# One layer of a hybrid sparse and dilated attention decoder: part of VectorE's work moved later in its queue, and the down projection's products regrouped by stationary operand

## The chip, the cores and the metric

The kernel runs on one core of a Trainium2 chip. The metric is the device time of one execution in microseconds (us), median over runs. The kernel before was run three times: 410.62 us median, 409.74 to 410.94. One further execution was profiled, and all rows below come from it.

## The reference, cut to what matters

```python
# x: (1, 256, 1024) float32; D_FF = 2816; 8 + 12 heads of 64 columns
h = rmsnorm(x, g_mix)
proj = h @ w_in                     # 5656 columns: q_a, kv_a, gate_a, qkv_b, merge_logits
kc = compress(kv_a[:, :, 0], pe_cmp_k, w_cmp_k1, w_cmp_k2)   # gelu(blocks @ w1) @ w2
vc = compress(kv_a[:, :, 1], pe_cmp_v, w_cmp_v1, w_cmp_v2)
gate_a = sigmoid(gate_a)
o_a = nsa_attention(q_a, kc, vc, ..., gate_a)                # compressed + selected + window
o_b = dilated_attention(qkv_b)
mixed = sigmoid(ga) * (o_a @ w_proj_nsa) + sigmoid(gb) * (o_b @ w_proj_dil)
x = x + mixed @ w_out
h = rmsnorm(x, g_ffn)
u, gate = split(h @ w_up)                                    # 2 x 2816 columns
x = x + (gelu(causal_conv3(u)) * gate) @ w_down
return rmsnorm(x, g_final)
```

## The kernel before, in words

**Three products for one.** Matmuls run in fp32r. Each operand is split into a high part (its fp32r copy, made by ScalarE) and a low part (the rest, a subtraction on VectorE), and a product is three matmuls: high by high, high by low, low by high. Names with h or hi (`whi`, `hTh`, `KH`, `ah`) are high parts, those with l or lo (`wlo`, `hTl`, `KL`, `al`) low parts.

**Units.** The weights are cut into 64 units, nearly all of 1 MB, in a list `units` that one loop (from L1084) goes through in order; i is the number of the unit. For unit i the loop starts the load of unit i+4 into one of three `raw` buffers, splits later units (`hi_of(i + 2)` on ScalarE, `lo_of(i + 1)` on VectorE, L128 and L132), issues the unit's matmuls (`u.mm`), and then its evacuation from PSUM (`u.evac`). Between these stand single steps under conditions on i. Nothing reorders afterwards: each engine carries its instructions out in the order in which the loop writes them, so a step that is written earlier delays all that is behind it on that engine. A `raw` buffer is loaded again when the low part of the unit in it is made.

**The units around the change.** Units 0 (the compression's keys and values) and 1 (the other keys of the first mixer), 2 (values and gates), 3 and 4 (`qa`, the queries of the first mixer), 5, 7 and 9 (`qb`, queries of the second), 6 and 8 (`w_cmp_k1` and `w_cmp_v1`, the compression's first layer, `mm_w1`, L421), 10 to 12 (`kb`). Steps among them:

- `ev_ka` (L384, unit 1's evacuation, called at i == 3): keys into `k`, four copies into `KH` (each group's keys in its own and in the other half of the partitions), two subtractions into `KL`.
- `xc_tile`, `split_cmp` (L325): high and low part of the compression's input, `XC`.
- `q_parts` (L436; L443 and L444): high and low part of the queries, `QS`, two heads of each group a call; `gates_of` (L429): the gates' sigmoid.
- `cmp_sum` (L721): adds the two halves of the compression's first layer (`ph`, in one of the two buffers of PSUM tag d) into `S2`; `cmp_fold` (L731) multiplies that on TensorE (L735).
- The first attention item, head 0, has its scores (`qk`, L840 and L842) behind unit 8, its softmax (`sm`, `sm2`, L854 to L873) on VectorE and ScalarE, and its transposes (`tr`, L882) behind unit 9.

PSUM tag d has two buffers. While `ph` holds one, units 5, 7 and 9 share the other, and each needs the evacuation (`ev_qb`, L450) of the one before.

**The feed-forward part.** From unit 31 on (`NFIRST`) the list is, for each j, two up units of 256 columns (weights stationary, `hTh` and `hTl` moving) and the down unit of j - 2 (activations `ah`, `al` stationary, weights moving). A down unit multiplies 256 rows of `w_down` into four PSUM banks (`ffn["y"]`: tiles `ps_s` and two `ps_t`), for two halves t of the sequence and two halves ch of the columns, in matmuls of 256 moving columns. `parts` (L160) writes the order: for each PSUM piece the products of `whi` with `ah` and `al` in turn (L177), and behind all pieces those of `wlo` (L182). `rt["kick"]` asks `parts` for one more matmul of 64 columns ahead of a unit (L172), whose result isn't used. The last two down units run piece by piece in `last` (L1180).

Of the kernel before, what the change touches and what calls it, by code (L numbers as in the profile page):

```python
# [14 lines left out]
AF = mybir.ActivationFunctionType  # L15
# [6 lines left out]
NF = DFF // 256  # L22
# [71 lines left out]
def build(ctx, tc, a, out):  # L94
# [67 lines left out]
    def parts(groups, w_stationary=True, start=True, stop=True):  # L162


        banks = set()
        kick = rt.pop("kick", None)
        if kick:

            (wh, _, xh, _), po = groups[0][2][0], groups[0][1]
            l, r = (wh, xh) if w_stationary else (xh, wh)  # L170
            po = pd([64], kick) if len(kick) == 1 else po[:, :64]
            T.matmul(po, l, r[:, :64], start=True, stop=True, skip_group_check=True)  # L172
        for (bank, po, ks) in groups:
            for (wh, wl, xh, xl) in ks:
                for x in (xh, xl):
                    l, r = (wh, x) if w_stationary else (x, wh)
                    T.matmul(po, l, r, start=start and bank not in banks, stop=False, skip_group_check=True)  # L177
                    banks.add(bank)
        for (bank, po, ks) in groups:
            for n, (wh, wl, xh, xl) in enumerate(ks):  # L180
                l, r = (wl, xh) if w_stationary else (xh, wl)
                T.matmul(po, l, r, start=False, stop=stop and n == len(ks) - 1, skip_group_check=True)  # L182

    def w3(u, k):
        n = u.n // k
        return (u.hi[:, u.o:u.o + u.n].rearrange("p (k c) -> p k c", k=k),
                u.lo[:, u.o:u.o + u.n].rearrange("p (k c) -> p k c", k=k))
# [40 lines left out]
    def bc(R, n):  # L228
        return R[:, None, :].to_broadcast([128, n, R.shape[-1]])
# [154 lines left out]
    def ev_ka(u):  # L384
        k = att.tile([128, 2, S], F32, name="E", tag="E", bufs=2)
        V.tensor_tensor(out=k, in0=u.p, in1=bc(rt["R"], 2), op=OP.mult)
        for g in range(2):
            h = slice(g * 64, g * 64 + 64)
            o = slice(64 - g * 64, 128 - g * 64)
            A.activation(KH[h, g], k[h], AF.Copy)  # L390
            V.tensor_sub(KL[h, g], k[h], KH.bitcast(F32)[h, g])
            A.activation(KH[o, g], k[h], AF.Copy)

    units.append(Unit(2048, lambda u: None, ev_ka))

# [40 lines left out]
    def q_parts(i):  # L436
        for g in range(2):
            h = slice(g * 64, g * 64 + 64)
            o = slice(64 - g * 64, 128 - g * 64)
            for j in (2 * i, 2 * i + 1):  # L440

                q, f = g * 4 + j, 1.0 / SLOPE_A[g * 4 + j]
                A.activation(M["QS"][h, q], qa[h, j], AF.Copy, scale=f)  # L443
                V.scalar_tensor_tensor(M["QS"][o, q], qa[h, j], f, M["QS"].bitcast(F32)[h, q],  # L444
                                       op0=OP.mult, op1=OP.subtract)
# [167 lines left out]
        return f  # L613

    def mm_down_part(u, j, tcs, c0=0, c1=512, own=None):
        wh, wl = w3(u, 2)
        h, l = ffn["a", j]
        parts([((t, ch), ffn["y"][t][ch][:, b:e] if own is None else own,
                [(wh[:, kt, ch * 512 + b:ch * 512 + e], wl[:, kt, ch * 512 + b:ch * 512 + e],
                  h[:, kt, t * 128:t * 128 + 128], l[:, kt, t * 128:t * 128 + 128]) for kt in range(2)])  # L620
               for (t, ch) in tcs for b, e in ([(0, 256), (256, 512)] if c1 - c0 == 512 else [(c0, c1)])],
              False, start=j == (0 if own is None else NF - 2), stop=j == NF - 1)

    def mm_down(j):
        def f(u):
            if j == 0:
                s2 = pd([2, 512], "s")
                ta = pd([512], "t")
                tb = pd([512], "t")
                ffn["y"] = [[s2[:, 0], s2[:, 1]], [ta, tb]]  # L630
            if j < NF - 2:
                rt["kick"] = "od"[j % 2]
                mm_down_part(u, j, [(t, ch) for t in range(2) for ch in range(2)])
        return f

# [368 lines left out]
    def load_to(n):  # L1004
        nonlocal loaded
        while loaded < min(n, len(units)):
            load_unit(units[loaded])
            loaded += 1
# [71 lines left out]
    def at(i):  # L1080
        return items.get(i, [])

    post = []
    for i, u in enumerate(units):  # L1084
        load_to(i + LA)
        for it in at(i - 3):
            it.fin()
        for it in at(i - 2):
# [18 lines left out]
        if i == 3:  # L1107
            hi_of(5)
            mixer_tiles()
            u1.evac(u1)  # L1110
            xc_tile()
            split_cmp(0)
            split_cmp(1)
        if i == 5:
            q_parts(0)
            gates_of()
        if i == 6:
            q_parts(1)
        if i == 9:
            cmp_sum()  # L1120
        if i == 11:
            cmp_kv_ev()
        if i == 14:
# [37 lines left out]
            u.pre(u)  # L1161
        if u.evac and i not in (0, 1, NFIRST):
            u.evac(u)
        if u.pre:
            post.append(post_g(len([q for q in units[:i] if q.pre])))
        for it in at(i - 2):
# [72 lines left out]
```

## Time and profile before

| | |
|---|---|
| median of 3 runs | 410.62 us |
| lowest, highest | 409.74, 410.94 us |
| profiled execution, its own time | 411.17 us |
| its span (first to last instruction) | 409.4 us |
| TensorE busy | 397.6 us, 97% |
| VectorE busy | 291.1 us, 71% |
| ScalarE busy | 212.2 us, 52% |
| mean granted TensorE clock | 0.991 of 2.4 GHz |

The difference of 1.77 us between the profiled execution's time and its span lies before its first and behind its last instruction. Matmuls are pipelined: one takes some 280 ns from start to end, and the next starts some 115 ns after it, so the distance from start to start is the cost, not the mean duration.

### The profile page before, as it was taken

The page shows a single profiled execution, that of the slowest core. Times are in us where ns is not written, and L with a number is a line of the kernel's source. Part 1 is how long each engine was busy: PE and PEld are TensorE (multiplying, and loading weights), DVE is VectorE, ACT ScalarE, POOL GpSimd, SP SyncE. Part 2 cuts the span into 40 slices and gives each one's busy share as a digit, 9 for nine tenths or more (in the row PEclk, how much of TensorE's full clock was granted, in tenths as well). Part 3 has the DMA queues.
Part 4 walks back from the last instruction along what each step waited for, and adds up shares of the span by engine and source line. Part 5 has one row for each costly group of instructions (what it writes and reads, how often), then busy time and mean ns, then how long its engine had stood idle before and what let it go on. Part 6 is the DMA issues. An engine that isn't in the chain of part 4 may idle for free.

```text
span 409.4 us, 8037 instructions
## 1 busy us (share of the span) xinstructions
PE 397.6 (97%) x3421; PEld 386.2 (94%) x3421; DVE 291.1 (71%) x486; ACT 212.2 (52%) x293; POOL 31.2 (8%) x58
## 2 busy tenths in 40 slices
PE   9999899999999999999999999999999999999993
PEld 6999898999998989999999999999999999999992
DVE  5878977887686756648889399685584764946853
ACT  6768552457654534681652766355255452653512
POOL 7100000000000000042143000000000000000012
PEclk9999899999999999999999999999999999999997
DMA  8963764324632343252555436753735727448002
GB/s 316 391 242 113 285 219 162 148 103 170 243 105 102 118 161 135 104 207 104 206 207 191 170 113 227 279 208 108 302 110 200 245 99 275 146 162 290 21 2 102
DMA packets 10980, 72.59 MB, mean 177 GB/s; under 512 B 1216, under 2 KB 1472, under 8 KB 2880
## 3 DMA queue, kind: packets, MB, share of 16 engines
q1 hardware_dynamic: 10512, 70.96, 47.4%
q10 hardware_dynamic: 432, 1.11, 0.8%
q8 instruction: 27, 0.44, 0.4%
q14 instruction: 9, 0.07, 0.1%
HBM read 71.02 MB, written 1.05 MB: 176 GB/s over the span
## 4 chain that ended last, share of the span: by engine, by line
PE 75%; DVE 14%; DMA 5%; ACT 3%; issue 2%; POOLq 0%; SPq 0%; POOL 0%; ACTq 0%; DVEq 0%
PE ps_d L177 24%; PE ps_d L182 12%; PE ps_o L177 9%; DVE wlo L132 5%; PE ps_s L177 5%; PE ps_t L177 5%; PE ps_o L182 5%; DMA raw<-in_wts_dram 4%; PE ps_s L182 3%; PE ps_t L182 2%; DVE hTl L202 2%; PE ps_o L895 2%; PE ps_s L936 1%; PE ps_d L280 1%; PE ps_t L882 1%
## 5 line engine op out<-in xcount | busy, mean ns | idle before, releaser
L132 DVE TENSOR_TENSOR wlo<-raw,whi 128x2048 fp32r<-128x2048 f32 (+2 forms) x61 | 135.2, 2218 | 4.6 <-ACT whi L128 4.6
L128 ACT ACTIVATE whi<-raw 128x2048 fp32r<-128x2048 f32 (+1 forms) x61 | 114.8, 1883 | 36.3 <-DMA raw<-in_wts_dram 32.4
L177 PE MATMUL ps_d<-hTh,whi 128*128 128x256 f32 x384 | 91.7, 283 | 1.8 <-DVE qb L450 1.8
L177 PE MATMUL ps_d<-hTl,whi 128*128 128x256 f32 x384 | 90.6, 281 | 0.0
L177 PEld LDWEIGHTS ps_d<-hTh,whi 128*128 128x128 f32 x384 | 73.4, 191 | 3.6 <-issue 3.3
L177 PEld LDWEIGHTS ps_d<-hTl,whi 128*128 128x128 f32 x384 | 73.4, 191 | 0.0
L182 PE MATMUL ps_d<-hTh,wlo 128*128 128x256 f32 x384 | 47.9, 278 | 0.8 <-DVE wlo L132 0.8
L182 PEld LDWEIGHTS ps_d<-hTh,wlo 128*128 128x128 f32 x384 | 45.7, 188 | 1.0 <-DVE wlo L132 1.0
L177 PE MATMUL ps_o<-hTh,whi 128*128 128x256 f32 x160 | 36.9, 277 | 0.0
L177 PE MATMUL ps_o<-hTl,whi 128*128 128x256 f32 x160 | 36.8, 277 | 0.0
L581 ACT ACTIVATE C<-U,small 128x256 f32<-128x256 f32 x22 | 12.0, 594 | 44.4 <-DVE U L577 44.4
L177 PEld LDWEIGHTS ps_o<-hTl,whi 128*128 128x128 f32 x160 | 30.1, 188 | 0.0
L177 PEld LDWEIGHTS ps_o<-hTh,whi 128*128 128x128 f32 x160 | 30.1, 188 | 0.0
L585 DVE SCALAR_TENSOR_TENSOR C<-U,small,C 128x256 f32<-128x256 f32 x44 | 19.4, 483 | 7.5 <-ACT C L581 7.4
L177 PE MATMUL ps_s<-whi,ah 128*128 128x256 f32 x88 | 22.1, 290 | 0.0
L859 ACT ACTIVATE E<-E,ast 128x256 f32<-128x256 f32 (+1 forms) x32 | 14.2, 444 | 14.6 <-DVE ast L854 14.6
L177 PE MATMUL ps_s<-whi,al 128*128 128x256 f32 x88 | 21.3, 281 | 0.0
L577 DVE TENSOR_TENSOR U<-ps_d,R 128x512 f32<-128x512 f32 x6 | 4.1, 689 | 23.1 <-PE ps_d L182 19.3
L177 PE MATMUL ps_t<-whi,ah 128*128 128x256 f32 x84 | 20.4, 281 | 0.0
L177 PE MATMUL ps_t<-whi,al 128*128 128x256 f32 x84 | 20.4, 281 | 0.0
L132 POOL TENSOR_TENSOR wlo<-raw,whi 128x1024 fp32r<-128x1024 f32 x3 | 7.8, 2584 | 158.8 <-ACT whi L128 158.8
L182 PE MATMUL ps_o<-hTh,wlo 128*128 128x256 f32 x160 | 19.8, 277 | 0.0
(273 smaller groups left out, 768.1 us busy)
## 6 DMA issues: line engine op xcount, KB each, us to landing
raw<-in_wts_dram SPq DMA_DIRECT2D x61, 1024.0 KB, 4.8
first<-in_first_dram SPq DMA_DIRECT2D x2, 768.0 KB, 7.8
raw<-in_wts_dram SPq DMA_DIRECT2D x1, 1120.0 KB, 10.6
xn<-in_xn_dram SPq DMA_DIRECT2D x2, 512.0 KB, 12.0
xT<-in_xT_dram SPq DMA_DIRECT2D x1, 1024.0 KB, 7.0
first<-in_first_dram SPq DMA_DIRECT2D x2, 384.0 KB, 5.2
gf<-in_g_final_dram ACTq DMA_DIRECT2D x1, 512.0 KB, 3.7
out_dram<-X SPq DMA_DIRECT2D x1, 512.0 KB, 2.6
```

The source lines that it names most:

```text
L128: A.activation(u.hi[:, u.o + c0:u.o + c1], u.raw[:, c0:c1], AF.Copy)
L132: (eng or V).tensor_sub(u.lo[:, u.o + c0:u.o + c1], u.raw[:, c0:c1], u.hi.bitcast(F32)[:, u.o + c0:u.o + c1])
L177: T.matmul(po, l, r, start=start and bank not in banks, stop=False, skip_group_check=True)
L182: T.matmul(po, l, r, start=False, stop=stop and n == len(ks) - 1, skip_group_check=True)
L202: V.scalar_tensor_tensor(hTl[:, kt], x, g[:, kt:kt + 1], hTh.bitcast(F32)[:, kt], op0=OP.mult, op1=OP.subtract)
L280: T.matmul(u.p[:, i], l[:, kt, i * 128:i * 128 + 128], r[:, kt], start=kt == 0 and i == 0 and q == 0, stop=kt == 7 and q == 2, skip_group_ ...
L577: V.tensor_tensor(out=U[:, :, 2:], in0=u.p, in1=bc(rt["R2"], 2), op=OP.mult)
L581: A.activation(C[:, c], U[:, c, 2:], AF.Identity, scale=CW(2, t), bias=CB[:, t:t + 1])
L585: V.scalar_tensor_tensor(C[:, c], U[:, c, w:w + S], CW(w, t), C[:, c], op0=OP.mult, op1=OP.add)
L859: A.activation(self.E[:, i], self.E[:, i], AF.Exp, bias=mn[:, i:i + 1], scale=-1.0, accum_out=dn[:, i:i + 1])
L882: T.transpose(p[:, i], self.E[:, 4 * c + 2 * g + b, k * 128:(k + 1) * 128], ident)
L895: T.matmul(oA[js[c]][g * 64:g * 64 + 64, t * 128:(t + 1) * 128], Vn[:, k, b * 128 + g * 64:b * 128 + g * 64 + 64], self.PT[:, i], start=t ...
```

## The change

Part 1 moves steps of units 3 to 9. The keys' `KL` subtractions and the copies into the other half of `KH` become a function of their own, `split_keys`, called at i == 4. `u1.evac` is called behind the `split_cmp` pair. The two `q_parts` calls go from before the matmuls of units 5 and 6 to behind the evacuations of units 6 and 7, `gates_of` behind the second. `cmp_sum` goes to the head of the loop's body at i == 9.

Part 2 rewrites `mm_down_part`. Its loops are now: which product (`whi` by `ah`, `whi` by `al`, `wlo` by `ah`), t, kt, and inside these ch and the halves of 256 columns, so that four matmuls in a row have the same stationary operand and write four different pieces of PSUM. The number of matmuls is the same. The down units no longer ask for the kick.

```diff
     def ev_ka(u):
         k = att.tile([128, 2, S], F32, name="E", tag="E", bufs=2)
         V.tensor_tensor(out=k, in0=u.p, in1=bc(rt["R"], 2), op=OP.mult)
+        xr["k"] = k
+        for g in range(2):
+            A.activation(KH[g * 64:g * 64 + 64, g], k[g * 64:g * 64 + 64], AF.Copy)
+
+    def split_keys():
+        k = xr["k"]
         for g in range(2):
             h = slice(g * 64, g * 64 + 64)
-            o = slice(64 - g * 64, 128 - g * 64)
-            A.activation(KH[h, g], k[h], AF.Copy)
+            A.activation(KH[64 - g * 64:128 - g * 64, g], k[h], AF.Copy)
             V.tensor_sub(KL[h, g], k[h], KH.bitcast(F32)[h, g])
-            A.activation(KH[o, g], k[h], AF.Copy)
...
     def mm_down_part(u, j, tcs, c0=0, c1=512, own=None):
         wh, wl = w3(u, 2)
         h, l = ffn["a", j]
-        parts([((t, ch), ffn["y"][t][ch][:, b:e] if own is None else own,
-                [(wh[:, kt, ch * 512 + b:ch * 512 + e], wl[:, kt, ch * 512 + b:ch * 512 + e],
-                  h[:, kt, t * 128:t * 128 + 128], l[:, kt, t * 128:t * 128 + 128]) for kt in range(2)])
-               for (t, ch) in tcs for b, e in ([(0, 256), (256, 512)] if c1 - c0 == 512 else [(c0, c1)])],
-              False, start=j == (0 if own is None else NF - 2), stop=j == NF - 1)
+        half = [(0, 256), (256, 512)] if c1 - c0 == 512 else [(c0, c1)]
+        start, seen = j == (0 if own is None else NF - 2), set()
+        for n, (w, x) in enumerate(((wh, h), (wh, l), (wl, h))):
+            for t in sorted({t for t, _ in tcs}):
+                for kt in range(2):
+                    for ch in [ch for q, ch in tcs if q == t]:
+                        for b, e in half:
+                            T.matmul(ffn["y"][t][ch][:, b:e] if own is None else own, x[:, kt, t * 128:t * 128 + 128],
+                                     w[:, kt, ch * 512 + b:ch * 512 + e], start=start and (t, ch) not in seen,
+                                     stop=j == NF - 1 and n == 2 and kt == 1, skip_group_check=True)
+                            seen.add((t, ch))
...
             if j < NF - 2:
-                rt["kick"] = "od"[j % 2]
                 mm_down_part(u, j, [(t, ch) for t in range(2) for ch in range(2)])
...
     for i, u in enumerate(units):
         load_to(i + LA)
+        if i == 9:
+            cmp_sum()
...
         if i == 3:
             hi_of(5)
             mixer_tiles()
-            u1.evac(u1)
             xc_tile()
             split_cmp(0)
             split_cmp(1)
-        if i == 5:
-            q_parts(0)
-            gates_of()
-        if i == 6:
-            q_parts(1)
-        if i == 9:
-            cmp_sum()
+            u1.evac(u1)
+        if i == 4:
+            split_keys()
...
         if u.evac and i not in (0, 1, NFIRST):
             u.evac(u)
+        if i in (6, 7):
+            q_parts(i - 6)
+        if i == 7:
+            gates_of()
```

VectorE, units 3 to 5, before (a name's number tells one tile of that name from another; `wlo_428` is unit 5's low part, the rows with `raw_345` are unit 6's, `qb_431<-ps_d_573` is unit 5's evacuation):

```order
L391 TENSOR_TENSOR KL_91<-E_434,KH_90 64x512 x2
L306 MEMSET XC_442 128x8 x4
L330 TENSOR_TENSOR XC_442<-PT_409,XC_442 128x2x256 x2
L368 SCALAR_TENSOR_TENSOR qa_87<-ps_t_451,R_379 128x512
L132 TENSOR_TENSOR wlo_428<-raw_343,whi_427 128x2048
L368 SCALAR_TENSOR_TENSOR qa_87<-ps_t_504,R_379 128x512
L410 TENSOR_TENSOR whi_553<-raw_345,whi_553 128x8x128
L410 TENSOR_TENSOR wlo_554<-raw_345,wlo_554 128x8x128
L444 SCALAR_TENSOR_TENSOR QS_430<-qa_87,QS_430 64x256 x4
L431 TENSOR_SCALAR gates_86<-gates_86 128x48
L432 RECIPROCAL gates_86<-gates_86 128x48
L450 SCALAR_TENSOR_TENSOR qb_431<-ps_d_573,scB_94,R_379 128x256 x2
```

and with the change (lines below the diff's first part have other numbers: L396 is `KL`, L414 the compression weights' low parts, L454 `ev_qb`):

```order
L306 MEMSET XC_434 128x8 x4
L330 TENSOR_TENSOR XC_434<-PT_409,XC_434 128x2x256 x2
L386 TENSOR_TENSOR E_443<-ps_d_246,R_379 128x512
L368 SCALAR_TENSOR_TENSOR qa_87<-ps_t_447,R_379 128x512
L132 TENSOR_TENSOR wlo_428<-raw_343,whi_427 128x2048
L396 TENSOR_TENSOR KL_91<-E_443,KH_90 64x512 x2
L368 SCALAR_TENSOR_TENSOR qa_87<-ps_t_504,R_379 128x512
L414 TENSOR_TENSOR whi_553<-raw_345,whi_553 128x8x128
L414 TENSOR_TENSOR wlo_554<-raw_345,wlo_554 128x8x128
L454 SCALAR_TENSOR_TENSOR qb_431<-ps_d_562,scB_94,R_379 128x256 x2
```

Two `KL` subtractions now stand behind unit 5's low part instead of ahead of it, and four `QS` subtractions and the gates are gone from between unit 6's low parts and unit 5's evacuation.

VectorE, from the end of head 0's softmax to unit 9's evacuation, before (`wlo_737` is unit 10's low part):

```order
L867 RECIPROCAL ast_747<-ast_747 128x4
L870 TENSOR_TENSOR ast_747<-ast_747,gates_86 128x4
L873 TENSOR_SCALAR E_746<-E_746,ast_747 128x256 x4
L132 TENSOR_TENSOR wlo_737<-raw_627,whi_736 128x2048
L728 TENSOR_TENSOR S2_764<-ps_d_638,S2_764 64x256
L450 SCALAR_TENSOR_TENSOR qb_431<-ps_d_767,scB_94,R_379 128x256 x2
```

and with the change, from unit 7's evacuation to the start of that softmax (L454 `ev_qb`, L448 `QS`, L435 and L436 the gates, `wlo_702` unit 9's low part, L738 `cmp_sum`):

```order
L454 SCALAR_TENSOR_TENSOR qb_431<-ps_d_652,scB_94,R_379 128x256 x2
L448 SCALAR_TENSOR_TENSOR QS_430<-qa_87,QS_430 64x256 x4
L435 TENSOR_SCALAR gates_86<-gates_86 128x48
L436 RECIPROCAL gates_86<-gates_86 128x48
L132 TENSOR_TENSOR wlo_702<-raw_558,whi_701 128x2048
L738 TENSOR_TENSOR S2_746<-ps_d_619,S2_746 64x256
L864 ISA E_749,ast_750<-ps_s_739,tab_103 128x256
```

`S2` has moved from behind head 0's softmax and unit 10's low part to ahead of that softmax, and the second four `QS` and the gates stand behind unit 7's evacuation, ahead of unit 9's low part.

TensorE, the end of an up unit and the start of the first down unit, before:

```order
L177 MATMUL ps_d<-hTl,whi 128x256
L182 MATMUL ps_d<-hTh,wlo 128x256 x16
L172 MATMUL ps_o<-whi,ah 128x64
L177 MATMUL ps_s<-whi,ah 128x256
L177 MATMUL ps_s<-whi,al 128x256
```

and with the change, the whole unit (`ps_s` is t = 0, `ps_t` t = 1):

```order
L182 MATMUL ps_d<-hTh,wlo 128x256 x16
L630 MATMUL ps_s<-whi,ah 128x256 x8
L630 MATMUL ps_t<-whi,ah 128x256 x8
L630 MATMUL ps_s<-whi,al 128x256 x8
L630 MATMUL ps_t<-whi,al 128x256 x8
L630 MATMUL ps_s<-wlo,ah 128x256 x8
L630 MATMUL ps_t<-wlo,ah 128x256 x8
```

The matmul of 64 columns is gone, and the products with `ah` and `al` no longer alternate.

## Rows read from the trace of the kernel before

**Rows 1.** The page, parts 1 and 2: busy time of each engine, and one row of the 40 slices (granted clock, in tenths).

```profile
PE 397.6 (97%) x3421; PEld 386.2 (94%) x3421; DVE 291.1 (71%) x486; ACT 212.2 (52%) x293; POOL 31.2 (8%) x58
...
PEclk9999899999999999999999999999999999999997
```

**Rows 2.** Busy time by stretches of 20 us: TensorE's matmuls, its weight loads, VectorE, ScalarE, GpSimd (instructions in brackets), granted clock, share of the DMA engines, GB/s.

```profile
40.00:60.00 20.00, 18.20 (x138) 17.84 (x138) 17.20 (x36) 12.07 (x19) 0.00 (x0) 0.91 0.73 263
60.00:80.00 20.00, 19.30 (x169) 18.23 (x169) 16.13 (x38) 7.76 (x15) 0.00 (x0) 1.00 0.45 159
```

**Rows 3.** TensorE in order of time, 34.9 to 63.3 us: start, duration (us), line, operands; in brackets the idle time before it and what ended that.

```profile
34.92 0.28 PE L177 MATMUL ps_d<-hTh,whi 128*128 128x256 f32 x1
...
38.43 0.28 PE L177 MATMUL ps_d<-hTl,whi 128*128 128x256 f32 x1
39.47 2.10 PE L182 MATMUL ps_d<-hTh,wlo 128*128 128x256 f32 x16 [0.76 <-DVE wlo L132]
...
45.40 0.36 PE L177 MATMUL ps_d<-hTh,whi 128*128 128x256 f32 x1 [1.80 <-DVE qb L450]
...
47.32 0.42 PE L177 MATMUL ps_d<-hTh,whi 128*128 128x256 f32 x1
...
52.58 1.15 PE L421 MATMUL ps_d<-whi,XC 128*64 128x256 f32 x8
53.57 1.15 PE L421 MATMUL ps_d<-wlo,XC 128*64 128x256 f32 x8
...
55.49 0.28 PE L177 MATMUL ps_d<-hTh,whi 128*128 128x256 f32 x1
...
60.95 1.03 PE L882 MATMUL ps_t<-ident,E 128*128 128x128 f32 x8
62.68 0.63 PE L735 MATMUL ps_o<-E,S 64*128 64x32 f32 x4 [0.70 <-DVE S L728]
63.24 0.39 PE L177 MATMUL ps_d<-hTh,whi 128*128 128x256 f32 x1
```

**Rows 4.** VectorE in order of time, 31 to 63 us, same columns.

```profile
31.34 0.69 DVE L386 TENSOR_TENSOR E<-ps_d,R 128x512 f32<-128x512 f32 x1
32.73 0.68 DVE L391 TENSOR_TENSOR KL<-E,KH 64x512 fp32r<-64x512 f32 x1 [0.70 <-ACT KH L390]
34.02 0.69 DVE L391 TENSOR_TENSOR KL<-E,KH 64x512 fp32r<-64x512 f32 x1 [0.61 <-ACT KH L390]
...
35.32 1.29 DVE L330 TENSOR_TENSOR XC<-PT,XC 128x512 fp32r<-128x512 f32 x2 [0.45 <-ACT XC L329]
...
39.94 1.21 DVE L410 TENSOR_TENSOR whi<-raw,whi 128x1024 fp32r<-128x1024 f32 x1
...
42.31 1.54 DVE L444 SCALAR_TENSOR_TENSOR QS<-qa,QS 64x256 fp32r<-64x256 f32 x4
...
44.48 0.78 DVE L450 SCALAR_TENSOR_TENSOR qb<-ps_d,scB,R 128x256 f32<-128x256 f32 x2
...
55.77 0.42 DVE L854 CUSTOM_DVE_ANT_0 E<-ps_s,tab 128x256 f32<-128x256 f32 x1
...
60.02 2.28 DVE L132 TENSOR_TENSOR wlo<-raw,whi 128x2048 fp32r<-128x2048 f32 x1
62.22 0.41 DVE L728 TENSOR_TENSOR S<-ps_d,S 64x256 f32<-64x256 f32 x1
```

**Rows 5.** The page, part 6: the loads of the units, with KB each and the median us from issue to landing.

```profile
raw<-in_wts_dram SPq DMA_DIRECT2D x61, 1024.0 KB, 4.8
```

**Rows 6.** The chain that ended last, in order of time: start us, us, what. Unit 7 (45.40), units 13 and 14 (87.85, 95.42: activations stationary, weights moving), the last product of units 17 and 36 (125.44, 250.15: weights stationary), part of the first down unit (253.96, 255.85) and the up unit behind it.

```profile
45.40 5.53 PE ps_d L177 x32
...
87.85 3.77 PE ps_d L177 x32
...
95.42 3.64 PE ps_d L177 x32
...
125.44 1.88 PE ps_d L182 x16
...
250.15 1.81 PE ps_d L182 x16
...
253.96 1.89 PE ps_t L177 x16
255.85 0.94 PE ps_s L182 x8
...
257.73 3.65 PE ps_o L177 x32
```

**Rows 7.** TensorE in order of time where the first down unit begins.

```profile
251.80 0.19 PE L172 MATMUL ps_o<-whi,ah 128*128 128x64 f32 x1
251.83 0.36 PE L177 MATMUL ps_s<-whi,ah 128*128 128x256 f32 x1
252.03 0.28 PE L177 MATMUL ps_s<-whi,al 128*128 128x256 f32 x1
252.15 0.28 PE L177 MATMUL ps_s<-whi,ah 128*128 128x256 f32 x1
```

**Rows 8.** The page, part 5: weight loads of the first two products of the units that write `ps_d`, in which each `whi` tile is stationary for two matmuls in a row (with `hTh`, then with `hTl`); count, then busy us and mean ns of one, idle time before.

```profile
L177 PEld LDWEIGHTS ps_d<-hTh,whi 128*128 128x128 f32 x384 | 73.4, 191 | 3.6 <-issue 3.3
L177 PEld LDWEIGHTS ps_d<-hTl,whi 128*128 128x128 f32 x384 | 73.4, 191 | 0.0
```

## The prediction, made before the changed kernel ran

> **What bounds the kernel now.** I read the page first: TensorE is busy 97% of the span, VectorE 71% [rows 1]. So what counts is time that TensorE loses, by idling, by a lower clock, or by a slower pace than it could have. The row of the granted clock has one dip in the body, in the fifth slice of the span, and the stretches of 20 us put it between 40 and 60 us (mean 0.91), where VectorE is at its fullest, 17.20 of 20 us [rows 1, 2]. TensorE's order in time shows why [rows 3]: three waits, each on VectorE. At 39.47 unit 5's third product waits for its low weights. At 45.40 unit 7 waits for `qb`, the evacuation of the PSUM buffer that it shares with unit 5. At 62.68 the fold of the compression waits for `S2`. Behind the second wait the clock falls to its lower level, 1.2 of 2.4 GHz: at 47.32 a matmul takes 0.42 us that elsewhere takes 0.28, and unit 7's first 32 matmuls take 5.53 us where a unit at full clock takes 3.65 [rows 3, 6]. Behind 63 us the chain of waits runs through TensorE but for a stretch ahead of the feed-forward part, where VectorE's steps themselves hang on TensorE's results; so a shift of TensorE at 63 us passes on to the end.
>
> In the feed-forward part TensorE never idles; there only its pace counts. Up units start a matmul every 1.81/16 = 113 ns, down units every 1.89/16 = 118 ns [rows 6].
>
> **Part 1, VectorE's order.** It adds and removes no instruction and issues no DMA; SP's and GpSimd's orders stay. I lay the new order out from 31.34 us, where the two orders part, with durations of rows 3, 4 and 6.
>
> TensorE without waits and at full clock: unit 5 starts at 34.92 and takes 48 x 113 ns = 5.44, to 40.36. Unit 6 takes 2 x (53.57 - 52.58) = 1.98, to 42.34; unit 7 5.44, to 47.78; unit 8 and head 0's scores 55.49 - 52.58 = 2.91, to 50.69; unit 9 5.44, to 56.13. The transposes and the fold take 63.24 - 60.95 = 2.29, less the wait at 62.68 with its start, 0.86: 1.43. Unit 10 would start at 57.56 and not at 63.24, so what is lost there now is 5.68. It is 0.92 for the first wait (39.47 - 38.43 less one step of 0.11), 2.0 for the second (1.80 idle, and a start that drags 0.2), 1.88 for the clock, 0.86 for the third [rows 3, 6].
>
> VectorE: before, unit 5's evacuation stood 44.48 - 31.34 = 13.14 behind the keys. Now four `QS` and the gates are behind it (44.48 - 42.31 = 2.17 less), and the waits of 0.70, 0.61 and 0.45 for ScalarE's high parts go, since the `XC` pair now goes first, whose input is long there, and `KL` stands behind a low part of 2.2 us in which ScalarE makes `KH`: 40.55 [rows 4]. It ends at 41.3, and unit 7 needs it at 42.34. Unit 5's low part, with the two `KL` (1.37) and the waits out of its way, ends at about 36.3 and is needed at 38.5. Then: unit 7's low part 2.2, to 43.5; `QS` 1.6, to 45.1; unit 8's two low parts 42.31 - 39.94 = 2.37, to 47.5, needed at 47.78; unit 7's evacuation when its matmuls are done, 47.9 to 48.7; `QS` and gates 2.2, to 50.9; unit 9's low part 2.2, to 53.1, needed at 54.3; `S2` 0.4, to 53.5; head 0's softmax 60.02 - 55.77 = 4.25, to 57.7 [rows 4].
>
> So one **new wait** takes the place of the three: the transposes behind unit 9 want the softmax, TensorE is there at 56.1, and its last input at 57.7. Some five transposes of 0.11 and the fold, 0.56 [rows 3], stand behind that: unit 10 starts at 58.9 with a dragging start. Part 1 is worth 63.24 - 58.9 = **4.4 us**. Its upper end is 5.7, if nothing waited. Its lower end is 2.5, if the clock falls once more (1.88). Behind that, unit 10's low part ends at 59.9, needed at 62.5, and VectorE's next steps have slack while TensorE runs ahead by 2 us more than VectorE does.
>
> The loads go with the buffers: unit 8's buffer is free at 36.3, and 4.8 us later its weights are there [rows 5]; ScalarE has their high parts at 43 and the first `QS` high parts by 43.4, when VectorE comes to `QS`. Unit 10's is free at 43.5, landed at 48.3, wanted at 58.9. That is cover, but the `QS` hang on it by some tenths.
>
> **Part 2, the down units.** 48 matmuls a unit stay, and in the tail too. Gone are nine kicks: from the kick's start to the third start behind it are 252.15 - 251.80 = 0.35 us, where two steps of 0.118 would be 0.24 [rows 7]. 9 x 0.11 = **1.0 us**. If the first real matmul dragged as the one behind the kick does (0.20 against 0.12), 0.3 would be left; up units follow one another without that.
>
> Does the stationary operand's order change the pace? The trace has both orders. Units that write `ps_d` keep a piece of `whi` for two matmuls in a row, and load it twice all the same: 384 loads ahead of `hTh` and 384 ahead of `hTl`, of the same length [rows 8]. So "kept" drops no load, and the number of loads stays 48 a unit. Nor is 113 or 118 bound to an order: unit 13 runs its 32 matmuls in 3.77, unit 14, of the same form, in 3.64; unit 17's third product, all different stationary operands, has 1.88, unit 36's 1.81 [rows 6]. As far as I can read it, a unit keeps the pace with which it comes in. All down units now come in behind a kick and run at 118. For the pace I take 118, no gain, since every down row has it; the other bound is 113: 11 x 48 = 528 matmuls x 4.5 ns = 2.4 us.
>
> The Trainium skill, page "TensorE: Matmul & The Clock Gate", section "Back-to-back issue gap", has a matmul of N columns every N / 2.4 GHz + 2.5 ns, which is 109 ns for 256 columns, but says that in a stream loads and matmuls set the distance together. By the first, the down units could gain 528 x 9 ns = 4.7 us and the time would be 400.5, an estimate; the trace does not agree, since its fastest units of 256 columns keep 113 ns [rows 6].
>
> The sum: the profiled execution took 411.17 us. 411.17 - 4.4 - 1.0 = 405.8. The median of the runs shown is 0.55 below that execution, so the forecast for the median is **405.2 us**.
>
> **The rivals.** *The down units take the fast pace* (30%). For it: without the kick a down unit follows an up unit at 113 without a stop, and unit 14 shows that the form can run so. Against: unit 13. 405.2 - 2.4 = 402.8.
>
> *The clock falls again* (10%), at the new wait of 1.5 us, or already before it if the `QS` come late. For it: it fell behind the 1.80; against: it did not behind the 0.70 at 62.68 [rows 2, 3]. 405.2 + 1.9 = 407.1.
>
> *The up units fall to 118* (7%), because they now follow a down unit without the pattern that the kick set. 20 x 48 x 4.5 ns = 4.3: 409.5, no change that can be told. Against: the kick lies 48 matmuls ahead of the next up unit, which begins behind the same `wlo` products as now.
>
> *Slower* (6%): a matmul that takes up a new stationary operand behind a run of four pays the 0.20 of rows 7, since four matmuls into four pieces of PSUM let nothing be prepared. 12 runs x 11 units x 0.082 = 10.8: 416.0. It decides from 41 ns a run, where the 5.4 are gone. Against: now each matmul of the third product has a new operand, and pays nothing.
>
> That the change does not do what it says is the middle of my forecast for its second half: the operand stays in the order, not in the engine.
>
> **How the numbers follow.** Forecast 47%, fast down units 30%, the clock 10%, slow up units 7%, slower 6%. Units 10 to 23 now run partly at 118 and partly at 113, and which do may change: 0.2 us a unit (3.77 and 3.64 for the first two products of units 13 and 14, [rows 6]), so the forecast alone spreads by 1.5 either way. The range, 401.8 to 408.0, takes in the forecast, the fast down units and the clock; 13% lies outside by the last two cases. A measurement of this kernel can tell about 0.3%, 1.2 us. Faster is the forecast, the fast down units and the clock, 87%; same the slow up units, 7%; slower 6%.
>
> **What would show it.** Right: granted clock 1.00 between 40 and 60 us; no idle of TensorE ahead of unit 5's third product, of unit 7 and of the fold; a wait of some 1 to 1.5 us ahead of or among the transposes at 56 to 58; unit 10 at 58.9; as many loads as matmuls in the down units, at 118 ns; 48 x 0.118 = 5.66 us from a down unit's start to the next up unit's, where it is 0.35 + 46 x 0.118 = 5.77 now. Wrong: unit 10 later than 60, a down unit under 5.5 us, or up units over 5.5.

## The result, and the profile after

The changed kernel takes **406.20 us** (median of 4 runs, 405.66 to 406.50) where the kernel before takes 410.78 beside it (4 runs, 409.74 to 411.12): a ratio of 0.9899, with a 95% interval of 0.9880 to 0.9918. The forecast was 405.2. In a second group of runs it took 406.09 (6 runs, ratio 0.9897, 0.9872 to 0.9923). The profiled execution took 406.50 us, its span is 404.7.

The page of after, busy time and granted clock; the stretches of 20 us beneath (columns as in [rows 2]):

```profile
PE 394.7 (98%) x3412; PEld 383.2 (95%) x3412; DVE 291.2 (72%) x486; ACT 212.4 (52%) x293; POOL 31.2 (8%) x58
...
PEclk9999999999999999999999999999999999999997
```

```profile
40.00:60.00 20.00, 18.96 (x155) 18.15 (x155) 17.55 (x36) 13.73 (x25) 0.00 (x0) 1.00 0.61 215
60.00:80.00 20.00, 20.00 (x178) 19.21 (x177) 17.37 (x41) 8.73 (x14) 0.00 (x0) 1.00 0.46 159
```

Nine matmuls and nine weight loads fewer, still as many loads as matmuls (3412 of each). The dip of the clock is gone (1.00 where [rows 2] have 0.91), and TensorE idles 1.04 us between 40 and 60 us instead of 1.80.

TensorE of after in order of time, as in [rows 3]:

```profile
35.30 0.28 PE L177 MATMUL ps_d<-hTh,whi 128*128 128x256 f32 x1
...
38.93 1.98 PE L182 MATMUL ps_d<-hTh,wlo 128*128 128x256 f32 x16
40.75 1.15 PE L425 MATMUL ps_d<-whi,XC 128*64 128x256 f32 x8
...
42.73 0.28 PE L177 MATMUL ps_d<-hTh,whi 128*128 128x256 f32 x1
...
57.62 1.46 PE L892 MATMUL ps_t<-ident,E 128*128 128x128 f32 x8 [0.90 <-DVE E L883]
59.01 0.63 PE L745 MATMUL ps_o<-E,S 64*128 64x32 f32 x4
59.57 0.39 PE L177 MATMUL ps_d<-hTh,whi 128*128 128x256 f32 x1
```

The waits of unit 5's third product (38.93), of unit 7 (42.73) and of the fold (59.01) are gone. One is new, 0.90 us ahead of the transposes. VectorE of after, as in [rows 4]:

```profile
33.76 2.28 DVE L132 TENSOR_TENSOR wlo<-raw,whi 128x2048 fp32r<-128x2048 f32 x1
35.96 1.40 DVE L396 TENSOR_TENSOR KL<-E,KH 64x512 fp32r<-64x512 f32 x2
...
40.95 0.88 DVE L454 SCALAR_TENSOR_TENSOR qb<-ps_d,scB,R 128x256 f32<-128x256 f32 x2 [0.60 <-PE ps_d L182]
...
48.40 0.88 DVE L454 SCALAR_TENSOR_TENSOR qb<-ps_d,scB,R 128x256 f32<-128x256 f32 x2 [0.41 <-PE ps_d L182]
...
53.61 0.40 DVE L738 TENSOR_TENSOR S<-ps_d,S 64x256 f32<-64x256 f32 x1
...
57.12 1.14 DVE L883 TENSOR_SCALAR E<-E,ast 128x256 f32<-128x256 f32 x4
```

Now VectorE waits for TensorE, 0.60 and 0.41 us ahead of the two evacuations, and `S2` (53.61) and the softmax's end (58.26) set the transposes.

The chain of waits of after where the first down unit lies, as in [rows 6]:

```profile
248.32 0.94 PE ps_s L630 x8
249.26 0.94 PE ps_t L630 x8
...
253.03 0.94 PE ps_t L630 x8
253.97 3.65 PE ps_o L177 x32
257.62 1.81 PE ps_o L182 x16
```

Eight matmuls in 0.94 us are 118 ns each, as before, and the up unit behind keeps its 3.65 and 1.81 us.

**Where the time went.** Three marks divide every trace: unit 5's first matmul, unit 10's, and that of the first down unit with its kick; the last column runs to the end of TensorE's last matmul. In us:

| | unit 5 starts | to unit 10 | to the first down unit | to the end |
|---|---|---|---|---|
| before | 34.92 | 28.32 | 188.56 | 150.56 |
| after | 35.30 | 24.27 | 188.59 | 149.55 |
| difference | +0.38 | -4.05 | +0.03 | -1.01 |

They add up to the 4.66 by which TensorE's last matmul ends earlier (397.71 against 402.37), but for rounding. The +0.38 lies ahead of everything that the change touches: unit 3's first matmul has it already, 24.42 against 24.04. Over all traces of this study unit 5 starts between 34.51 and 35.30. The +0.03 says that units 10 to 23, whose paces the prediction let vary, took as long as before.

### The profile page after: what moved, and what is told of

Same layout as the page of the kernel before. It is cut to its first block, busy times and chain, and to the rows that moved or that the text cites. A ratio compares the mean times of both kernels' runs of the same rounds, so it can differ in the third digit from the quotient of the medians.

```text
span 404.7 us, 8015 instructions
## 1 busy us (share of the span) xinstructions
PE 394.7 (98%) x3412; PEld 383.2 (95%) x3412; DVE 291.2 (72%) x486; ACT 212.4 (52%) x293; POOL 31.2 (8%) x58
## 3 DMA queue, kind: packets, MB, share of 16 engines
q10 hardware_dynamic: 432, 1.11, 0.7%
## 4 chain that ended last, share of the span: by engine, by line
PE 83%; DVE 10%; ACT 2%; DMA 2%; issue 1%; SPq 0%; POOLq 0%; POOL 0%; ACTq 0%
PE ps_d L177 25%; PE ps_d L182 12%; PE ps_o L177 9%; PE ps_s L630 8%; PE ps_t L630 7%; PE ps_o L182 5%; DVE wlo L132 4%; DMA first<-in_first_dram 2%; PE ps_t L177 2%; DVE hTl L202 2%; PE ps_d L344 2%; PE ps_o L905 2%; PE ps_s L946 1%; PE ps_t L892 1%; PE ps_d L280 1%
## 5 line engine op out<-in xcount | busy, mean ns | idle before, releaser
L177 PE MATMUL ps_d<-hTh,whi 128*128 128x256 f32 x384 | 90.1, 280 | 0.0
L177 PE MATMUL ps_d<-hTl,whi 128*128 128x256 f32 x384 | 89.0, 277 | 0.0
L177 PEld LDWEIGHTS ps_d<-hTh,whi 128*128 128x128 f32 x384 | 72.2, 188 | 1.7 <-issue 1.3
L177 PEld LDWEIGHTS ps_d<-hTl,whi 128*128 128x128 f32 x384 | 72.2, 188 | 0.0
L585 ACT ACTIVATE C<-U,small 128x256 f32<-128x256 f32 x22 | 12.0, 595 | 44.1 <-DVE U L581 44.1
L182 PEld LDWEIGHTS ps_o<-hTh,wlo 128*128 128x128 f32 x160 | 18.9, 188 | 0.0
L581 DVE TENSOR_TENSOR U<-ps_o,R 128x512 f32<-128x512 f32 x5 | 3.4, 689 | 17.6 <-PE ps_o L182 17.6
L1207 POOL TENSOR_TENSOR tiny<-cst,tiny 128x1 f32<-128x1 f32 x2 | 1.4, 696 | 170.6 <-ACT sq L1206 170.6
L366 DVE TENSOR_TENSOR ML<-ps_d,R 128x512 f32<-128x512 f32 x8 | 5.5, 692 | 12.3 <-PE ps_d L182 12.3
```

The costliest lines, as they stand in the source:

```text
L581: V.tensor_tensor(out=U[:, :, 2:], in0=u.p, in1=bc(rt["R2"], 2), op=OP.mult)
L585: A.activation(C[:, c], U[:, c, 2:], AF.Identity, scale=CW(2, t), bias=CB[:, t:t + 1])
```

## The experiments

Three groups of runs, each with the kernel before beside it: medians 410.21 us (32 runs), 410.91 (18) and 410.28 (12). The table has the median of each, and the three stretches of its one profiled execution with that execution's own time. Kernels of a group, and stretches of any traces, compare closely; medians of different groups do not below half a microsecond.

| | group | us (runs) | ratio, 95% interval | profiled | to unit 10 | to down | to end |
|---|---|---|---|---|---|---|---|
| e1 order only | 1 | 407.61 (9) | 0.9942, 0.9917 to 0.9967 | 407.48 | 24.27 | 188.82 | 150.57 |
| e2 down units only | 1 | 409.38 (12) | 0.9976, 0.9951 to 1.0001 | 409.95 | 28.27 | 188.59 | 149.55 |
| e3 no kick, old order | 1 | 408.51 (12) | 0.9974, 0.9948 to 0.9999 | 408.46 | 26.79 | 188.81 | 149.55 |
| e4 kick put back | 1 | 407.38 (12) | 0.9931, 0.9909 to 0.9952 | 407.37 | 24.27 | 188.59 | 150.57 |
| e0 changed kernel | 2 | 406.09 (6) | 0.9897, 0.9872 to 0.9923 | 406.27 | 24.27 | 188.58 | 149.55 |
| e5 sum late | 2 | 409.13 (12) | 0.9964, 0.9942 to 0.9986 | 409.10 | 25.77 | 190.19 | 149.54 |
| e6 queries early | 2 | 405.77 (7) | 0.9899, 0.9863 to 0.9936 | 410.72 | 26.36 | 191.10 | 149.55 |
| e8 second queries late | 2 | 404.89 (6) | 0.9865, 0.9838 to 0.9893 | 406.18 | 23.24 | 189.89 | 149.54 |
| e7 keys early | 3 | 408.69 (7) | 0.9963, 0.9948 to 0.9977 | 410.20 | 26.54 | 190.17 | 149.54 |
| e9 wide down units | 3 | 407.33 (6) | 0.9938, 0.9916 to 0.9959 | 408.71 | 24.27 | 190.21 | 150.58 |
| e10 e8 and e9 | 3 | 406.22 (5) | 0.9901, 0.9883 to 0.9919 | 406.75 | 22.78 | 189.21 | 150.58 |
| e11 three starts | 3 | 407.78 (1) | | 407.78 | 24.27 | 188.60 | 151.19 |

### The two halves of the change

**e1**: after, with the old `mm_down_part` and `rt["kick"] = "od"[j % 2]`.

> Only part 1 of the change; down units in the old order, with their kicks. Theory (part 1 is worth the 3.6 us by which unit 10 starts earlier, and nothing of part 2 depends on it): 410.8 - 3.6 = 407.2 us, unit 10 at about 59.6 us in the span, down units 5.77 us each from start to the next up unit. Rival (the regrouped order does more than drop the kicks, some of the 4.6 us is its own): 408 us or more. Rival (part 1 gives all 4.6): 406.2.

**e2**: before, with the new `mm_down_part` and without that line.

> Only part 2: the old order on VectorE, down units regrouped and without kicks. Theory (nine kicks of 0.117 us are all it is worth): 410.8 - 1.05 = 409.7 us, down units 5.65 us, 118 ns a matmul, unit 10 at 63.2, the clock down between 46 and 50 us as before. Rival (the kept operand quickens the down units when nothing else is changed): 113 ns a matmul, 5.44 us a unit, 408.5 or less.

**e3**: before, and nothing but

```diff
-                rt["kick"] = "od"[j % 2]
```

> The kernel before with the nine kicks of the down units left out and nothing else; the products keep their old order, alternating between the two stationary operands. Theory (the kick is the whole of part 2, the order of the products is worth nothing): 409.7 us, the same as with the regrouped order within 0.3, down units 5.65 us. Rival (without a kick the old order drags at its start or sets the following up units at 118 ns, which is why there was a kick): between 410.8 and 414.

**e4**: after, with

```diff
+                po = pd([64], "od"[j % 2])
+                T.matmul(po, ffn["a", j][0][:, 0, :128], w3(u, 2)[0][:, 0, :64], start=True, stop=True, ...)
                 mm_down_part(u, j, [(t, ch) for t in range(2) for ch in range(2)])
```

> The changed kernel with a matmul of 64 columns put back ahead of each of the nine regrouped down units. Theory (the kick costs 0.117 each time whatever the order behind it): 406.2 + 1.05 = 407.2 us, down units 5.77 us. Rival (the kick costs only where the old order follows it): 406.2.

The last stretch settles part 2: 150.56 or 150.57 with kicks, 149.55 without, in either order of the products. **The nine kicks are worth 1.01 us, the regrouping by stationary operand nothing.** e1 and e4 say the same in time, 407.61 and 407.38. The medians of e2 and e3, 409.38 and 408.51, lie apart although their last stretches are the same. The runs of each are of two kinds (below), and six of twelve are of the upper kind in e2, five in e3. Besides, e2's lower runs are 0.4 us above e3's; none of them was profiled, and that stays open. Part 1 is the first stretch, 24.27 in every trace that has it whole.

e3 brought something that no theory held. It waits at unit 7 as the kernel before does [rows 3], and its clock does not fall. TensorE of e3 there, and VectorE's evacuation of unit 5:

```profile
44.91 0.36 PE L177 MATMUL ps_d<-hTh,whi 128*128 128x256 f32 x1 [1.80 <-ACT whi L405]
```

```profile
43.99 0.78 DVE L450 SCALAR_TENSOR_TENSOR qb<-ps_d,scB,R 128x256 f32<-128x256 f32 x2
```

The view names a step of ScalarE as what ended the wait, but it is the same wait: the evacuation ends at 44.77, 0.14 us ahead of the matmul, as in the kernel before (45.26 and 45.40, [rows 3, 4]). The stretch of e3 from 40 to 60 us, columns as in [rows 2]:

```profile
40.00:60.00 20.00, 18.20 (x150) 17.65 (x148) 18.56 (x36) 12.31 (x20) 0.00 (x0) 1.00 0.71 261
```

The same 1.80 us of idle time, a clock of 1.00, and a first stretch of 26.79 where before and e2, with the fall, have 28.32 and 28.27. So **the fall is not the wait's fixed price: it comes in some executions and not in others**, and costs 1.5 us here. The runs of the kernel before fit that: of 62 in these groups 28 lie between 409.15 and 409.92, and 34 above 410.6. e3 has runs at 408.3 to 408.6, at 409.8 to 410.1 and one at 412.99, and its profiled one (408.46) is of the lower kind; e2's (409.95, with the fall) is of the upper of its two. Only for these executions does a trace show it; in the others it is inferred. The mean granted clock of each run bears it out for most of them. A fall like that of [rows 2] takes 0.09 of 20 us, 1.8 us or 0.004 of the span. The 28 lower runs have 0.994 to 0.998; of the 34 upper ones 23 have 0.990 to 0.993 and seven 0.994, which allows a fall, but four have 0.996 or 0.997, too high for one like this (0.998 - 0.004 = 0.994). What made those four slower no trace shows.

### Which of part 1's moves counts

**e0**: the changed kernel itself.

> The changed kernel again, for its spread beside the others of this group. What the runs of the kernel before suggest: its times lie in two groups, 409.3 to 409.7 and 410.7 to 411.4 us, and in one profiled execution of a kernel with the old order on VectorE unit 7 kept the full clock behind its wait. Theory (the clock falls behind the wait of unit 7 in some executions only, and that makes the two groups): 406.2 us, mostly one group. Rival (the new wait ahead of the transposes lets the clock fall in some executions too, as the order-only kernel's three runs at 408.6 beside six at 407.4 hint): a second group some 1.2 us above, at about 407.4, in a quarter of the executions.

Five runs at 405.87 to 406.27, one at 407.51. Neither of the two traces of this kernel (after's and e0's) has a fall behind the new wait, but e9's does, which has the same VectorE order (below), and the run at 407.51 has a granted clock of 0.993 where the other five have 0.994 to 0.998. So the rival has something to it, though the second group is one run of six here.

**e5**: after, with

```diff
-        if i == 9:
-            cmp_sum()
         for it in at(i - 3):
...
+        if i == 9:
+            cmp_sum()
         if i == 11:
```

> The changed kernel, with only the compression sum S2 back in its old place, behind head 0's softmax and unit 10's low part. Theory (its move removes a wait of the fold): softmax ends 0.4 earlier, unit 10's low part then ends at about 60.0 and S2 at 60.5, the fold waits some 2 us instead of 0, unit 10 starts at about 61.2 instead of 59.6: 406.2 + 1.6 = 407.8 us, or 409.3 where the clock falls as well. Rival (the transposes and the fold wait for the same stretch of VectorE's work, so its place in that stretch is worth nothing): 405.8 to 406.2.

TensorE of e5 at the fold:

```profile
60.02 0.63 PE L745 MATMUL ps_o<-E,S 64*128 64x32 f32 x4 [1.76 <-DVE S L738]
```

As the theory had it: two runs at 407.5 and 407.6, ten from 408.8 up, and in the profiled one the clock is 0.91 between 60 and 80 us. Moving `cmp_sum` is worth 1.5 us, and 1.5 more where the clock falls.

**e6**: after, with `q_parts(0)`, `gates_of()` and `q_parts(1)` back ahead of the matmuls of units 5 and 6.

> The changed kernel, with only the queries' low parts and the gates back in their old places, ahead of the evacuations of units 5 and 6. Theory (the waits are not additive: TensorE waits ahead of the transposes for a VectorE that is busy throughout, so a wait of 0.6 to 2 us that comes back at unit 7 is paid only by what exceeds those 1.1): unit 7 starts 0.6 to 2 us later, the wait ahead of the transposes shrinks by as much, unit 10 at 59.6 to 60.5: 406.2 to 407.1 us. Rival (each wait is paid in full, as the prediction added them up: 2.0 for this one): 408.2, and 410.1 where the clock falls.

Six of seven runs take 405.42 to 405.94, so undoing this move costs nothing and may give 0.3 us. The seventh, 410.72, is the one that was profiled; there a load came late and the clock fell (0.83 between 60 and 80 us), so its stretches say nothing of the move (ScalarE of e6, at unit 10's high part):

```profile
52.49 1.92 ACT L128 ACTIVATE whi<-raw 128x2048 fp32r<-128x2048 f32 x1 [5.81 <-DMA raw<-in_wts_dram]
```

Up to that load the trace does show what the move does. Unit 7 waits 0.42 us for VectorE again, but VectorE, which now works where it waited in after, begins unit 9's low part 14.74 us behind unit 5's start (49.66 - 34.92) instead of 16.17 (51.47 - 35.30). That the softmax gains by this what unit 7 loses is likely and not shown, since the late load comes between.

**e7**: after, with

```diff
+            u1.evac(u1)
+            split_keys()
             xc_tile()
             split_cmp(0)
             split_cmp(1)
-            u1.evac(u1)
-        if i == 4:
-            split_keys()
```

> The changed kernel, with only the keys back in their old place: evacuation, copies and the two KL ahead of the XC pair. Theory (as with the queries: what comes back as a wait of unit 5's third product, 0.9, and of VectorE for ScalarE, 0.7 + 0.6 + 0.45, is paid only where VectorE has no slack of its own left; it idles 0.60 and 0.41 ahead of the two evacuations of qb): the third product of unit 5 waits some 0.9 us, unit 10 starts 0.3 to 0.8 later: 406.1 + 0.3 to 0.8 = 406.4 to 406.9 us. Rival (paid in full): 407.1 by the 0.92 alone, 407.9 by VectorE's 1.76.

Both were too low: 408.69, with six of seven runs between 408.61 and 408.85, is 2.5 us above the changed kernel's 406.2 (2.27 in the first stretch of the table). ScalarE of e7, at unit 8's high part:

```profile
44.32 1.06 ACT L409 ACTIVATE whi<-raw 128x1024 fp32r<-128x1024 f32 x1 [4.95 <-DMA raw<-in_wts_dram]
```

and VectorE, at unit 5's low part and at the first `QS`:

```profile
36.99 2.28 DVE L132 TENSOR_TENSOR wlo<-raw,whi 128x2048 fp32r<-128x2048 f32 x1
...
46.66 1.55 DVE L448 SCALAR_TENSOR_TENSOR QS<-qa,QS 64x256 fp32r<-64x256 f32 x4 [1.54 <-ACT QS L447]
```

Unit 5's low part begins at 36.99 where after has 33.76. It frees the `raw` buffer of unit 8, whose load lands 4.8 us behind its end [rows 5], at some 44.1; ScalarE's high parts of unit 8 wait for that, the high parts of `QS` stand behind them, and VectorE waits 1.54 for those. That is the larger part of the cost, not all of it: VectorE is late by itself too, by 1.11 us at the first evacuation of `qb` (42.06 against 40.95), of which 0.7 are left when the 0.41 of slack ahead of the second are used up. These 0.7 are what the theory had (0.3 to 0.8). I had counted VectorE's and TensorE's direct waits and left out that the move sets a load.

The seventh run, 410.20, is again the profiled one, and its trace has the fall of the clock, behind a wait of 1.16 us ahead of the transposes (granted clock 0.91 between 60 and 80 us). The fall lies in the second stretch, 1.58 us longer than after's, and explains why this run is 1.5 us above the other six.

**e8**: after, with

```diff
-        if i in (6, 7):
-            q_parts(i - 6)
+        if i == 6:
+            q_parts(0)
         if i == 7:
             gates_of()
+        if i == 10:
+            q_parts(1)
```

> The changed kernel, with the second half of the queries' low parts (heads 2 and 3, not needed before the attention item behind unit 13) moved on from behind unit 7's evacuation to behind unit 10's. Theory (VectorE's work between unit 7's evacuation and the end of the softmax sets the wait ahead of the transposes): four QS of some 0.4 us gone from there, the softmax ends 1 to 1.6 us earlier, the transposes wait 0.1 at most, unit 10 starts at 58.5 instead of 59.6: 406.2 - 1.0 = 405.2 us, with no second group of times if that wait is what lets the clock fall. Rival (VectorE is as full behind unit 10, and the wait turns up there): 406.2 to 406.8.

The theory holds: **404.89 us, the fastest here**, 1.2 below the changed kernel of the same group. TensorE of e8, no idle time ahead of the transposes:

```profile
55.99 1.46 PE L892 MATMUL ps_t<-ident,E 128*128 128x128 f32 x8
57.38 0.63 PE L745 MATMUL ps_o<-E,S 64*128 64x32 f32 x4
57.94 0.39 PE L177 MATMUL ps_d<-hTh,whi 128*128 128x256 f32 x1
```

It has two kinds of run too (four at 404.59 to 405.02, two at 405.93 and 406.18), at clocks of 0.994 to 0.998 alike. The profiled one, 406.18, shows another cause, in its chain ahead of the first down unit:

```profile
225.30 3.85 PE ps_o L177 x32
229.15 1.88 PE ps_o L182 x16
...
242.34 3.77 PE ps_d L177 x32
246.11 1.89 PE ps_d L182 x16
```

These four up units run at 118 ns a matmul where after runs them at 113: 22.70 us for the four where after takes 21.87. That is 0.83 of the 1.30 us by which the second stretch is longer than after's. Another 0.42 lie between the starts of units 11 and 12 (8.74 us where after has 8.32; e10, with the same order, has 8.68), where the transposes of the next attention item stand. So the rival is right in part: some of what the first stretch gains is paid back behind unit 10.

### The pace of 113 and 118 ns

**e9**: after, with

```diff
-        half = [(0, 256), (256, 512)] if c1 - c0 == 512 else [(c0, c1)]
+        half = [(c0, c1)]
```

> The changed kernel, with the down units in matmuls of 512 columns instead of two of 256: half the matmuls and half the weight loads for the same columns. Theory (the loads lie beside the matmuls, the columns set the pace; the scores' matmuls of 512 columns start 233 to 236 ns apart, two of 256 in a down unit 236): 24 x 0.233 to 0.236 = 5.59 to 5.66 us a unit where it is 5.65 now: 405.4 to 406.1 us. Rival (each matmul pays something fixed for its own load, 118 ns being 256 columns at 2.4 GHz and 11 ns more, and half as many pay half): 24 x 0.224 = 5.39 us a unit, 11 units, 403.2 us.

The down units take what the theory says, 5.59 us (24 times 0.233), although half the loads are gone. The kernel is slower all the same, as the table's last stretch shows (150.58), and its chain behind the first down unit:

```profile
254.07 0.93 PE ps_t L630 x4
255.00 3.77 PE ps_o L177 x32
258.77 1.89 PE ps_o L182 x16
...
270.98 0.93 PE ps_t L630 x4
271.91 3.65 PE ps_d L177 x32
275.55 1.81 PE ps_d L182 x16
```

Every second pair of up units now runs at 118 ns, 0.41 us a pair. Neither expectation had that. Its trace also has the fall behind the new wait, in unit 10 (59.68 on), and the second stretch is 1.62 longer than after's:

```profile
57.09 1.46 PE L892 MATMUL ps_t<-ident,E 128*128 128x128 f32 x8 [0.90 <-DVE E L883]
...
59.50 0.38 PE L177 MATMUL ps_d<-hTl,whi 128*128 128x256 f32 x1
59.68 0.41 PE L177 MATMUL ps_d<-hTh,whi 128*128 128x256 f32 x1
```

**e10**: e8's and e9's edits together.

> The second half of the queries' low parts behind unit 10's evacuation, and the down units in matmuls of 512 columns. Theory (the two lie in different stretches and add up): 404.9 less what the wide down units give alone, 404.1 to 404.9 us. Rival (the pace of the up units behind them changes with it): 405 or more.

406.22: the rival. The first stretch keeps e8's gain (22.78), the last has e9's loss (150.58).

**e11**: after, with three ways to begin a down unit.

```diff
+                if j % 3:
+                    n = 256 if j % 3 == 1 else 128
+                    po = pd([n], "od"[j % 2])
+                    T.matmul(po, ffn["a", j][0][:, 0, :128], w3(u, 2)[0][:, 0, :n], start=True, stop=True, ...)
                 mm_down_part(u, j, [(t, ch) for t in range(2) for ch in range(2)])
...
-                        for b, e in half:
+                        for b, e in (half if seen or j % 3 or own is not None or j > 8 else [(0, 128), (128, 256), (256, 512)]):
```

> The changed kernel with three ways to begin a down unit, in turn: its first matmul in two of 128 columns (j = 0, 3, 6), an extra matmul of 256 columns ahead (j = 1, 4, 7), an extra one of 128 columns ahead (j = 2, 5, 8). Theory of the prediction (a unit keeps the pace with which it comes in): at least one of the three ways brings its units to 113 ns. Rival (118 ns belongs to the down units, however they begin): 118 ns in all nine, and 113 in the up units behind them.

This kernel was run once, and that execution profiled. The two extra matmuls leave 118. The split start brings its three units to 113 ns, and the up units behind them to 118, here for j = 0 and j = 1 in e11's chain:

```profile
247.87 1.03 PE ps_s L630 x9
248.90 0.91 PE ps_t L630 x8
...
253.43 3.77 PE ps_o L177 x32
257.20 1.89 PE ps_o L182 x16
...
264.86 0.94 PE ps_s L630 x8
...
270.51 3.64 PE ps_d L177 x32
274.16 1.81 PE ps_d L182 x16
```

So the pace belongs to neither the form nor the order: it is set where one form follows another, and the next such start sets it anew. (Two up units in a row keep one pace, in every trace here.) The gain was paid back fourfold: a split unit takes 5.56 us, with its 49 matmuls, instead of 5.65, and the two up units behind it 11.32 instead of 10.90.

## Why the prediction was right

**The waits.** Read rightly: three went, one came, at the place and of the size that was written (1.0 to 1.5 us; it is 0.90 of idle time and a slow first transpose). From unit 5 to unit 10 the forecast was 58.9 - 34.92 = 23.98 us; it is 24.27. Of the 0.29, VectorE has 0.18: counted from unit 5's start its softmax ends at 22.96 instead of 22.78, by small amounts in several steps. The other 0.11 lie behind that, 1.31 from the softmax's end to unit 10 instead of 1.2. The first evacuation begins 5.65 behind unit 5's start where 5.63 was forecast (40.55 - 34.92), and that was luck: I had VectorE arrive there just then, and in fact it was 0.60 early and waited for TensorE. The clock's fall was priced at 1.88 and measures 1.5, mostly since unit 7 without it ran at 118 ns in e3 and not at the 113 that I had set beside it. On the scale of the profiled executions 405.8 was forecast and 406.50 measured: 0.29 from here and 0.38 from the start of unit 5, which nothing in the change moves. The other 0.3 of the miss is the step from execution to median, 0.55 below for before and 0.30 for after.

**What part 1 is worth** depends on a choice that I did not see as one. Against an execution with the fall it is 4.05 us, against one without it 28.32 - 1.53 - 24.27 = 2.52. I took the profiled execution, which had the fall, for the kernel; about half of its runs are of the kind that is 1.5 us faster (medians 409.6 and 411.1 of the 28 and 34), where there is less to gain. The median of before in the first comparison, 410.78, happened to be of the upper kind, and so the sum came out. That was luck: against runs of the lower kind the same kernel gains 3.4 us, not the 5.4 of the sum.

**The sum of three waits** was a wrong account of causes, though its total held. Undone one at a time, the keys cost 2.3 to 2.5 us, the compression sum 1.5 to 3, the queries and gates nothing, although they stood ahead of the largest of the three waits (1.80 at unit 7). Waits in a row on one late engine are not separate prices: VectorE was late as a whole, and TensorE paid at whichever place it met it. The prediction called the load of unit 8 "cover" on which the `QS` hang "by some tenths"; e7 shows 1.54 us of VectorE's time, by way of a buffer that comes free 3.2 us sooner with the change, as much as the whole move of the sum is worth without a fall of the clock.

**Part 2.** The kicks: 1.0 forecast, 1.01 measured, and shown to be all of it by e3. One load to a matmul: as forecast (3412 of each). The pace of 118: as forecast. The rival of the fast down units (30%) failed: all nine down units of after begin behind units at 113 and run at 118, so the pace of the unit before does not carry over into a unit of the other form. That a unit keeps to its end the pace with which it begins is borne out by e11. Slow up units (7%) did not come, they keep 3.65 and 1.81 us; nor did a price for each new stationary operand (6%), since a down unit takes 5.65 us.

By the Trainium skill, page "TensorE: Matmul & The Clock Gate", section "Back-to-back issue gap", matmuls of 512 columns, each taken by itself, would follow one another every 512 / 2.4 + 2.5 = 216 ns at the full clock, an estimate; e9's matmuls of 512 columns have 233. The same section says that in a stream loads and matmuls set the distance together, and gives 131 ns for 512 columns there; e9's 233 does not agree with that figure. Halving the loads in e9 took 118 to 116.5 ns for 256 columns, so here the loads hardly set the distance.

**The clock again** (10%, 407.1) was rightly a rival: e9's trace shows it behind the 0.90, and it costs 1.6. In the changed kernel most runs are without it, by their times and clocks nine of ten.

Left open: what makes a unit's start set 113 or 118, whether a start can be found that gives 113 to up and down units alike (11 x 48 x 4.5 ns = 2.4 us for the down units), and what made the upper runs of which no trace was taken. In e1's three at 408.6 to 408.8 (granted clock 0.992, the other six 0.994 or more) and two of e4's (408.7, at 0.992 and 0.993) the clock speaks for a fall; e4's third, 409.05 at 0.997, has another cause.

## What to carry to other kernels

When one engine is late against another over a whole stretch, undo a reordering move by move before believing the list of waits: a move that only shifts the lateness is worth nothing (e6), and one that frees a load's buffer earlier can be worth more than the wait it was made for (e7). Give work that is wanted late (here the queries of heads 2 and 3) a place behind the stretch, not a later place within it (e8), and look at what it delays there. And look at several executions before pricing a fall of the clock, since one trace shows it as if it were certain.

## What the runs showed of the hardware

- Behind the same wait at unit 7 (1.80 us in before and e3) TensorE's clock fell to 1.2 GHz in the traces of before and e2 and stayed at 2.4 in e3's; behind the 0.90 ahead of the transposes it stayed in the traces of after, e0, e1, e4 and e11 and fell in e9's. It fell as well in e5 (behind 0.58 and 1.76 us of idle time), e6 (1.52) and e7 (1.16).
- In the feed-forward part of every trace here a stream of 128x256 fp32r matmuls keeps one of two paces, 113 or 118 ns, through a unit, its first few matmuls aside; splitting one matmul of 256 columns into two of 128 at its start (e11, three units of one execution) changed the pace of the unit to 113, and that of the 96 matmuls behind it to 118.
- Keeping a stationary operand for four matmuls saves no load (3412 loads to 3412 matmuls) and no time (149.55 us in e2 and e3), and half as many loads (512 columns a matmul, 233 ns, against two at 118) bring 1%.
